# Filter spectra whose one differing row is stored from a tile of its own, and matrix casts queued behind the splits of the turned input

## The chip, the cores and the metric

The kernel runs on one core of one Trainium2 chip. The metric is device time in microseconds of one execution. Three runs of the kernel before gave 2880.81, 2882.52 and 2874.01 us. The profile is of a further execution that took 2877.9 us.

The engines are called as in the profile: PE is TensorE's matrix multiply and PEld its weight load, DVE is VectorE, ACT is ScalarE, POOL is GpSimd, SP is SyncE, which issues transfers and computes nothing. "SPq" is a DMA issued from SP.

## What is computed

Two layers of a diffusion backbone over 1024 latent tokens and 256 context tokens, 1024 channels. The change lies in the even layer's Hyena half: a short convolution, then two long convolutions with filters that a small network generates. Both become products of spectra:

```python
def long_conv(u, filt, skip):
    L = u.shape[1]
    uf = jnp.fft.rfft(u, n=2 * L, axis=1)
    ff = jnp.fft.rfft(filt, n=2 * L, axis=0)
    y = jnp.fft.irfft(uf * ff[None], n=2 * L, axis=1)[:, :L]
    return y + u * skip

def hyena_mix(p, conv_w, conv_b, w1, b1, freq, w2, b2, w3, skip):
    L = p.shape[1]
    z = short_conv(p, conv_w, conv_b).astype(jnp.float32)
    x1, x2, v = jnp.split(z, 3, axis=-1)
    filt = hyena_filters(L, w1, b1, freq, w2, b2, w3)
    skip = skip.astype(jnp.float32)
    v = x1 * long_conv(v, filt[:, 0], skip[0])
    v = x2 * long_conv(v, filt[:, 1], skip[1])
    return v.astype(p.dtype)
```

The other half of the channels goes through a two-dimensional Fourier transform; each layer ends with a SwiGLU feed-forward part, and the odd layer does neighbourhood attention.

## The kernel before, in words

All products run on PE as fp32 in two parts: `split` (L345 to L351) makes a rounded high part `hi` on ACT (L349) and the remainder `lo` on DVE (L351), and a product is three matrix multiplies, hi by hi, hi by lo and lo by hi. Nearly every matrix multiply goes through the helper `mm` (L345), every SP transfer through `ld` (L330), every POOL transfer through `ldr` (L336).

**Order.** The program is written with generators that hand out pieces of work between matrix multiplies, and is then ordered by a scheduler that simulates a timeline (`schedule_with_timeline_sim=True`). So a small edit can change the order of instructions far away. Each engine's instructions then run in that fixed order. `follow(ins)` adds an order, no wait: what is issued inside it comes later on its own engine than `ins`.

**Filter spectra**, up to about 445 us. For each of the two long convolutions (o = 0, 1) the filter is turned into a spectrum for the latent tokens (`spectrum_l`) and one for the context tokens (`spectrum_c`). This runs as filler beside the input projection, with `short_conv` (L1044 to L1048, on ACT and DVE) and the Fourier part of the context (L1504 to L1512) beside it. For each block of 128 rows by 512 channels ACT copies the sum from PSUM to a tile `t` (L1018 in `spectrum_l`, L911 in `spectrum_c`), and `ld(d[eo], t)` stores it to DRAM. One block of each spectrum is stored a second time, as `d[2]`, with its row 0 replaced by the row for the highest frequency, `fpi`. For that DVE overwrites row 0 of the same tile `t` (L1023, L914), and the whole tile is stored again. The overwrite has to wait until the first store of `t` has landed. This happens four times: in `spectrum_l` at 195 and 302 us, in `spectrum_c` at 364 and 444 us. `d[2]` is read much later, in the combination of the spectra (`fr2`).

**The turned input.** After the spectra, `turned()` transposes the short convolution's output on PE: eight groups of four transposes (L1261), each group followed by `split` (ACT L349, DVE L351). Then eight calls of `unit(0, ...)` multiply the turned input by Fourier matrices. Such a matrix lies in DRAM as fp16, is loaded by SP into a `cs` tile and cast to fp32 by ACT: `cmat2` casts two matrices (L411), `cmat` one (L397). The first unit uses the split pairs as soon as they are there. `gate_rows` (L1277) and `turn_x` (L1288, L1290) prepare the gate of the same convolution beside it.

**SP's queue.** SP's DMAs are issued in order, and a transfer waits on SP for its operands, and for the landing of the SP transfer eight places earlier, whose semaphore it takes over. POOL's and ACT's queues do the same for a few other transfers.

Of the kernel before, what the change touches and what calls it, by code (L numbers as in the profile page):

```python
# [230 lines left out]
class Act:  # L231
# [3 lines left out]
    def __init__(self):  # L235
        self.t = {}
# [22 lines left out]
class Builder:  # L259
    def __init__(self, ctx, tc, a, out, taps=None, stop=None):  # L260
        self.tc, self.nc, self.a, self.out = tc, tc.nc, a, out
        self.taps, self.stop = taps, stop
        ent = ctx.enter_context
        self.cp = ent(tc.tile_pool(name="cp", bufs=1))
        self.p4 = ent(tc.tile_pool(name="p4", bufs=21))
        self.p2 = ent(tc.tile_pool(name="p2", bufs=35))
        self.pg = ent(tc.tile_pool(name="pg", bufs=4))
        self.pt = ent(tc.tile_pool(name="pt", bufs=6))
        self.pko = ent(tc.tile_pool(name="pk", bufs=4))
        self.pw = ent(tc.tile_pool(name="pw", bufs=2))  # L270
        self.pp = ent(tc.tile_pool(name="pp", bufs=6, space=bass.MemoryType.PSUM))
        self.pq = ent(tc.tile_pool(name="pq", bufs=2, space=bass.MemoryType.PSUM))
        self.dr = ent(tc.tile_pool(name="dr", bufs=1, space=bass.MemoryType.DRAM))
        self.pad(self.cp, PAD_C)
        self.k = self.mk = self.pk = 0
        self.mj = self.p3 = 0
        self.held = False
        self.banks = 8
        self.sq = {}

# [102 lines left out]
    def cmat(self, w, src, view=None, small=False, shift=False):  # L383

        if small:
            st, m = self.S2(F16), self.S2(F32R, w)
            self.ld(view(st[:, :w]) if view else st[:, :w], src)
            self.nc.scalar.copy(m, st[:, :w])
            return m
        st = self.W("ws", "cs", F16, w)  # L390
        self.ld(view(st) if view else st, src)
        if shift:
            self.mk ^= 1
            m = self.shifted(("wh", "wl")[self.mk], "mat", w)
        else:
            m = self.mat(w)
        self.nc.scalar.copy(m, st)  # L397
        return m

    def cmat2(self, src, shift=False):  # L400

        st = self.W("ws", "cs", F16, 2048)
        self.ld(st, src)
        out = []
        for j in (0, 1):
            if shift:
                self.mk ^= 1
                m = self.shifted(("wh", "wl")[self.mk], "mat")
            else:
                m = self.mat(1024)  # L410
            self.nc.scalar.copy(m, st[:, j * 1024:j * 1024 + 1024])  # L411
            out.append(m)
        return out

# [392 lines left out]
    def filter_sum(self, sq, o, raw):  # L807
# [40 lines left out]
        if sq == "c":  # L848
            nc.vector.scalar_tensor_tensor(kap, nrm, 0.5, self.skip[:, o * 4:o * 4 + 4], op0=MUL, op1=MUL)

    def spectrum_c(self, o, raw):
        nc, a = self.nc, self.a
        fe, fo, re = raw[(0, 0, 0)], raw[(0, 0, 1)], raw[(0, 1, 0)]
        tot = self.filter_sum("c", o, raw)
        fh = (self.S2(F32R), self.S2(F32R))
        nc.scalar.copy(fh[0][0:1, :], re[0:1, :])
        nc.vector.tensor_tensor(fh[1][0:1, :], re[0:1, :], fh[0][0:1, :].bitcast(F32), SUB)
        m0, m1 = self.mask[:, 0:1], self.mask[:, 1:2]
        alt, one = self.alt[:, 2:4], self.alt[0:1, 0:2]

        def operands():
            for i in range(4):
                if i == 0:
                    f0 = self.T()
                    nc.vector.tensor_copy(f0, fe)
                    nc.vector.tensor_tensor(f0[0:1, :], fe[0:1, :], fo[0:1, :], ADD)
                    nc.vector.tensor_scalar(f0[0:1, :], f0[0:1, :], 0.5, None, op0=MUL)
                f, r = raw[(0, 0, i // 2)], raw[(0, 1, i // 2)]
                t = self.T()
                if i == 0:  # L870
                    nc.vector.scalar_tensor_tensor(t, r, m0, f0, op0=MUL, op1=ADD)
                elif i == 1:
                    nc.vector.scalar_tensor_tensor(t, r, m1, f0, op0=MUL, op1=ADD)
                elif i == 3:
                    nc.vector.scalar_tensor_tensor(t, f, m0, r, op0=MUL, op1=ADD)
                else:
                    nc.gpsimd.tensor_tensor(t, f, r, SUB)
                xh, xl = self.S2(F32R), self.S2(F32R)
                self.split(t, xh, xl)
                mt = self.TK(F32R, 2 * P)  # L880
                self.ldr(mt, a["ff_c"][i, 0])
                yield xh, xl, mt
            yield None

        ops = operands()
        nxt = next(ops)
        yield
        for i in range(4):
            cls, eo = i % 2, i // 2
            if i == 0:  # L890
                fpi = self.PS()
            acc = self.PS()
            xh, xl, mt = nxt
            if i == 0:
                for j, x in enumerate((xh, xl)):
                    self.mm(fpi[0:2, :], alt, x, j == 0, False)
            nxt = next(ops)
            if i % 2 == 0:
                next(tot, None)
            self.mm(acc, mt[:, :P], xh, True, False)  # L900
            self.mm(acc, mt[:, :P], xl, False, False)
            self.mm(acc, mt[:, P:], xh, False, i != 0)
            if i == 0:
                for j in (0, 1):
                    self.mm(fpi[0:2, :], one, fh[j][0:1, :], False, j == 1)
                    self.mm(acc, self.sgn[0:1, 256:384], fh[j][0:1, :], False, j == 1)
            if ("c", o, cls, 0) not in self.frg:
                self.frg[("c", o, cls, 0)] = self.DR([3 if cls == 0 else 2, P, HC])
            d = self.frg[("c", o, cls, 0)]
            t = self.S2()  # L910
            nc.scalar.copy(t, acc)  # L911
            self.ld(d[eo], t)
            if i == 0:
                nc.vector.tensor_copy(t[0:1, :], fpi[0:1, :])  # L914
                self.ld(d[2], t)
            yield
        for _ in tot:
            pass

    def spectrum_l(self, o, raw, tot):  # L920

        nc, a = self.nc, self.a
        V = nc.vector
# [61 lines left out]
        for i in classes:  # L985
            cls, eo = i % 2, i // 2
            kept = []
            for p in (0, 1):
                if i + p == 0:
                    fpi = self.PS()  # L990
# [20 lines left out]
                for f in (0, 1):  # L1011
                    fb = 2 * p + f
                    if eo:
                        self.frg[("l", o, cls, fb)] = self.DR([3 if cls + fb == 0 else 2, P, HC])
                    d = self.frg[("l", o, cls, fb)]
                    if cls == 0 or p == 0:
                        t = self.S2()
                        nc.scalar.copy(t, accs[f])  # L1018
                        kept.append(t)
                    if cls == 0:  # L1020
                        self.ld(d[eo], t)
                        if i + fb == 0:
                            V.tensor_copy(t[0:1, :], fpi[0:1, :])  # L1023
                            self.ld(d[2], t)
                    elif p:
                        x, t = self.S2(), kept[f]
                        V.tensor_tensor(x, accs[f], t, ADD)
                        self.ld(self.frg[("l", o, 1, f)][eo], x)
                        V.tensor_tensor(t, *((t, accs[f]) if i == 1 else (accs[f], t)), SUB)
                        self.ld(d[eo], t)  # L1030
# [223 lines left out]
    def turned(self):  # L1254

        nc = self.nc
        self.tr = []
        for j in range(8):
            ps = self.PS()
            for cb in range(4):  # L1260
                last = nc.tensor.transpose(ps[:, cb * P:(cb + 1) * P], self.ab["l"][cb][:, j * P:(j + 1) * P], self.ident)  # L1261
            self.after_turned = last.ins
            hi, lo = self.S2(F32R), self.S2(F32R)
            self.split(ps, hi, lo)
            self.tr.append((hi, lo))
            yield

    def gate_rows(self, pc):
# [1607 lines left out]
```

## Time and profile before

| | |
|---|---|
| median of three runs | 2880.81 us (2874.01 to 2882.52) |
| profiled execution | 2877.9 us |
| its span, first to last instruction | 2876.1 us |
| PE busy | 2773.0 us, 96% |
| PEld busy | 2332.6 us, 81% |
| DVE busy | 2087.4 us, 73% |
| ACT busy | 1318.2 us, 46% |
| POOL busy | 545.1 us, 19% |
| mean granted TensorE clock | 0.980 |

Between the span and the profiled execution's own time lie 1.8 us that no instruction shows. PE is the bound on average, so a change counts where it lengthens or shortens the time in which PE stands or runs at a lower clock. In the timeline view a row gives the start, the time to the end of the group, the engine, the line, the operation, the tiles without their numbers and how many instructions were put together; the bracket is the idle time of the engine ahead of the row and what ended it.

### The profile page before, as it was taken

How to read it: one execution, taken by the hardware profiler on the slowest of the kernel's cores; microseconds unless marked ns; L12 is line 12 of the kernel's file. 1: busy time of each engine (PE TensorE's matmuls, PEld its weight loads, DVE VectorE, ACT ScalarE, POOL GpSimd, SP SyncE). 2: the span in 40 equal slices, each digit the busy share in tenths (PEclk: the TensorE clock that was granted, in tenths of full speed). 3: DMA queues.
4: the chain of work that ended last, by engine and by line, in shares of the span. 5: the costliest groups of instructions: out<-in, count | busy, mean ns of one | idle time of the engine just before them, and what ended most of it. 6: DMA issues, size and time to landing. Idle time of an engine off the chain costs nothing. (4 is left out here: it accounts for less than half of the span.)

```text
span 2876.1 us, 43702 instructions
## 1 busy us (share of the span) xinstructions
PE 2773.0 (96%) x15542; PEld 2332.6 (81%) x15542; DVE 2087.4 (73%) x3652; ACT 1318.2 (46%) x2270; POOL 545.1 (19%) x880
## 2 busy tenths in 40 slices
PE   6999899999999999999999999999999999999998
PEld 4867677788899888888888888888887788888887
DVE  6668787758787888966777537777777877765556
ACT  4434335543554333333455326777764533333434
POOL 2210234341001212222010002232222022112000
PEclk9999898999999999999999999999999999999999
DMA  7354546746556555658884436777866276434663
GB/s 266 119 170 164 161 130 201 236 153 238 203 186 218 195 202 194 217 189 330 309 312 152 146 123 158 189 175 186 228 212 225 101 251 223 154 110 166 230 196 133
DMA packets 298600, 557.35 MB, mean 194 GB/s; under 512 B 82056, under 2 KB 128842, under 8 KB 298382
## 3 DMA queue, kind: packets, MB, share of 16 engines
q1 hardware_dynamic: 234030, 364.19, 40.2%
q0 software_dynamic: 61504, 185.65, 18.4%
q10 hardware_dynamic: 2848, 4.72, 0.4%
q8 instruction: 123, 2.02, 0.3%
q14 instruction: 95, 0.78, 0.1%
HBM read 407.10 MB, written 119.80 MB: 183 GB/s over the span
## 5 line engine op out<-in xcount | busy, mean ns | idle before, releaser
L1908 PE MATMUL ps<-s,s 128*128 128x512 f32 x1976 | 489.0, 390 | 0.4 <-ACT g L1913 0.3
L1908 PEld LDWEIGHTS ps<-s,s 128*128 128x128 f32 x1976 | 371.7, 188 | 78.8 <-ACT g L1913 1.3
L345 PE MATMUL ps<-s,wh 128*128 128x256 f32 (+1 forms) x1784 | 412.1, 333 | 3.5 <-ACT s L349 1.1
L345 PEld LDWEIGHTS ps<-s,wh 128*128 128x128 f32 x1784 | 301.1, 192 | 38.5 <-ACT wh L349 2.1
L345 PE MATMUL ps<-s,wl 128*128 128x256 f32 (+1 forms) x892 | 275.1, 332 | 1.1 <-DVE wl L351 1.1
L351 DVE TENSOR_TENSOR wl<-ws,wh 128x1024 fp32r<-128x1024 f32 (+1 forms) x141 | 168.6, 1198 | 131.7 <-ACT wh L349 127.4
L2085 PE MATMUL ps<-s,s 128*128 128x512 f32 (+1 forms) x1000 | 259.7, 383 | 3.1 <-DVE s L351 3.0
L349 ACT CAST s<-s 128x1024 fp32r<-128x1024 f32 (+2 forms) x192 | 172.5, 927 | 192.6 <-DMA s<-d 177.2
L345 PE MATMUL pq<-s,wh 128*128 128x512 f32 (+1 forms) x840 | 256.1, 385 | 0.4 <-DVE s L914 0.4
L345 PE MATMUL ps<-s,s 128*128 128x65 f16 (+4 forms) x2748 | 229.6, 235 | 18.1 <-DMA s<-tk 12.3
L349 ACT CAST wh<-ws 128x1024 fp32r<-128x1024 f32 (+1 forms) x141 | 144.6, 1027 | 192.1 <-PE ps L345 86.4
L349 ACT CAST s<-t 128x512 fp32r<-128x512 f32 (+2 forms) x238 | 133.8, 582 | 213.5 <-PE ps L1908 71.4
L351 DVE TENSOR_TENSOR s<-s,s 128x1024 fp32r<-128x1024 f32 (+2 forms) x170 | 190.7, 1154 | 48.8 <-ACT s L349 46.3
L2085 PEld LDWEIGHTS ps<-s,s 128*128 128x128 f32 x1000 | 184.4, 188 | 41.2 <-DVE s L351 4.9
L351 DVE TENSOR_TENSOR s<-t,s 128x512 fp32r<-128x512 f32 (+2 forms) x238 | 151.2, 651 | 74.7 <-ACT s L349 53.1
L1908 PE MATMUL ps<-s,wh 128*128 128x512 f32 x616 | 191.3, 390 | 0.0
L345 PEld LDWEIGHTS ps<-s,wl 128*128 128x128 f32 x892 | 168.7, 192 | 19.3 <-DVE wl L351 2.4
L336 POOL DMA_DIRECT2D d<-s x186 | 101.5, 547 | 369.1 <-DVE s L1715 90.0
L345 PEld LDWEIGHTS pq<-s,wh 128*128 128x128 f32 x840 | 150.0, 190 | 22.2 <-DVE s L914 0.8
L345 PE MATMUL pq<-s,wl 128*128 128x512 f32 (+1 forms) x420 | 159.3, 379 | 0.0
L2085 PE MATMUL ps<-s 128*128 128x512 f32 (+1 forms) x500 | 150.8, 385 | 0.0
L345 PEld LDWEIGHTS ps<-s,s 128*128 128x128 f32 (+1 forms) x828 | 130.3, 193 | 22.8 <-issue 2.8
(491 smaller groups left out, 5557.3 us busy)
## 6 DMA issues: line engine op xcount, KB each, us to landing
s<-d SPq DMA_DIRECT2D x283, 256.0 KB, 3.9
d<-s POOLq DMA_DIRECT2D x170, 256.0 KB, 4.0
s<-in_down SPq DMA_DIRECT2D x150, 256.0 KB, 4.2
s<-in_ada_w POOLq DMA_DIRECT2D x64, 512.0 KB, 5.0
ws<-in_up SPq DMA_DIRECT2D x44, 512.0 KB, 3.8
d<-g POOLq DMA_DIRECT2D x86, 256.0 KB, 2.9
ws<-in_gate SPq DMA_DIRECT2D x42, 512.0 KB, 3.8
d<-tk POOLq DMA_DIRECT2D x66, 256.0 KB, 4.3
```

Of the source, the lines that this page charges most:

```text
L336: self.last_ldr = self.nc.gpsimd.dma_start(out, in_).ins
L345: self.last_mm = self.nc.tensor.matmul(o, l, r, start=st, stop=sp).ins
L349: self.last_hi = nc.scalar.copy(hi, src).ins
L351: self.last_lo = eng.tensor_tensor(lo, src, hi.bitcast(F32), SUB).ins
L1908: nc.tensor.matmul(ps, x[:, sl], y, start=first and j == 0 and x is wh and y is xh, stop=j == 3 and x is wl, skip_group_check=True)
L2085: m = nc.tensor.matmul(acc[j][:, c0:c1], x[:, sl], y[:, xs], start=first and k == 0, stop=last and k == 2, skip_group_check=True)
```

## The change

Two edits.

First, `other_row` makes the second stored copy without touching `t`. A `g` tile takes the row `fpi` (DVE, L857 after the change), rows 1 to 127 of `t` are stored to `d[2, 1:]`, and the row of its own to `d[2, 0:1]`. So at each of the four places the overwrite of `t` is gone, and one store of 128 rows becomes a store of 127 rows and one of 1 row.

Second, `turned()` notes the last `hi` of its splits, and the casts of `cmat` and `cmat2` are placed behind it on ACT. Before `turned()` there is nothing to place them behind.

```diff
@@ -275,6 +275,7 @@
+        self.turned_hi = None
@@ -394,7 +395,8 @@ (cmat)
-        self.nc.scalar.copy(m, st)
+        with self.follow(self.turned_hi):
+            self.nc.scalar.copy(m, st)
         return m
@@ -408,7 +410,8 @@ (cmat2)
-            self.nc.scalar.copy(m, st[:, j * 1024:j * 1024 + 1024])
+            with self.follow(self.turned_hi):
+                self.nc.scalar.copy(m, st[:, j * 1024:j * 1024 + 1024])
             out.append(m)
@@ -848,6 +851,13 @@
+    def other_row(self, d, t, fpi):
+
+        row = self.G()
+        self.nc.vector.tensor_copy(row[0:1, :], fpi[0:1, :])
+        self.ld(d[2, 1:], t[1:, :])
+        self.ld(d[2, 0:1], row[0:1, :])
+
@@ -911,8 +921,7 @@ (spectrum_c)
             if i == 0:
-                nc.vector.tensor_copy(t[0:1, :], fpi[0:1, :])
-                self.ld(d[2], t)
+                self.other_row(d, t, fpi)
@@ -1020,8 +1029,7 @@ (spectrum_l)
                         if i + fb == 0:
-                            V.tensor_copy(t[0:1, :], fpi[0:1, :])
-                            self.ld(d[2], t)
+                            self.other_row(d, t, fpi)
@@ -1263,6 +1271,7 @@ (turned)
             self.split(ps, hi, lo)
             self.tr.append((hi, lo))
+            self.turned_hi = self.last_hi
             yield
```

With its four more transfers SP has 1243 instead of 1239. Since the scheduler starts anew, other instructions move too: on PE the order differs from about 180 to 700 us and again in the last feed-forward part, from about 2440 us; between them it is the same.

The first place is SP in `spectrum_l` for o = 0, near 195 us. `d_398` is the spectrum, `s2_488` the tile `t`, the loads from `in_w3` bring the next filter weights (the array is called `in_w` in the profile). Before:

```order
L330 DMA d_398_1453<-s2_488_1780 128x512
L330 DMA s2_490_1788<-in_w3 128x512
L330 DMA s2_491_1790<-in_w3 128x512
L330 DMA d_401_1457<-s2_489_1785 128x512
L330 DMA d_398_1453<-s2_488_1780 128x512
```

And after the change:

```order
L331 DMA d_398_1453<-g_489_1783 1x512
L331 DMA d_398_1453<-s2_488_1780 128x512
L331 DMA d_398_1453<-s2_488_1780 127x512
L331 DMA s2_491_1790<-in_w3 128x512
L331 DMA s2_492_1792<-in_w3 128x512
```

The second store of the tile stood behind the two loads; its 127 rows now stand ahead of them.

The second place is SP in `spectrum_c` for o = 0, near 360 us. `d_872` (after: `d_874`) is the spectrum, `s2_885` (after: `s2_888`) the tile from which the Fourier part of the context works (DVE L1504, POOL L1506). Before:

```order
L330 DMA ws_958_3595<-in_w_in 128x1024
L330 DMA d_872_3238<-s2_874_3239 128x512
L330 DMA s2_885_3300<-d_91_293 128x256
L330 DMA d_872_3238<-s2_874_3239 128x512
L330 DMA ws_978_3688<-in_ada_w 128x1024
```

And after the change:

```order
L331 DMA ws_961_3601<-in_w_in 128x1024
L331 DMA d_874_3242<-g_877_3246 1x512
L331 DMA d_874_3242<-s2_876_3243 128x512
L331 DMA d_874_3242<-s2_876_3243 127x512
L331 DMA s2_888_3306<-d_91_293 128x256
L331 DMA ws_981_3694<-in_ada_w 128x1024
```

Here too the store of 127 rows has moved ahead of a load that stood before it.

The third place is ACT around the turned input, near 450 us. `mat<-cs` are the matrix casts, `s2<-ps` the `hi` parts of the eight turned splits, `s2<-pq` and `s2_1087<-ps` (L911) the copies of the last two spectrum blocks. Before:

```order
L411 CAST mat_1174_4429<-cs_1173_4427 128x1024
L411 CAST mat_1175_4431<-cs_1173_4427 128x1024
L911 COPY s2_1085_4152<-pq_1073_4124 128x512
L911 COPY s2_1087_4159<-ps_1086_4155 128x512
L349 CAST s2_773_2863<-s2_937_3503 128x256 x2
L349 CAST s2_775_2865<-s2_1023_3894 128x256 x2
L349 CAST s2_1099_4201<-ps_1098_4196 128x512
L411 CAST mat_1197_4517<-cs_1196_4515 128x1024
L349 CAST s2_1102_4210<-ps_1101_4205 128x512
L349 CAST s2_1105_4219<-ps_1104_4214 128x512
```

And after the change, from the second of those two copies on:

```order
L921 COPY s2_1091_4167<-ps_1090_4163 128x512
L350 CAST s2_775_2867<-s2_940_3509 128x256 x2
L350 CAST s2_777_2869<-s2_1026_3900 128x256 x2
L350 CAST s2_1103_4209<-ps_1102_4204 128x512
L350 CAST s2_1106_4218<-ps_1105_4213 128x512
L350 CAST s2_1109_4227<-ps_1108_4222 128x512
L350 CAST s2_1112_4236<-ps_1111_4231 128x512
L350 CAST s2_1115_4245<-ps_1114_4240 128x512
L350 CAST s2_1118_4254<-ps_1117_4249 128x512
L350 CAST s2_1121_4263<-ps_1120_4258 128x512
L350 CAST s2_1124_4272<-ps_1123_4267 128x512
L414 CAST mat_1178_4437<-cs_1177_4435 128x1024
```

All casts of matrices have moved behind the eighth turned split. At this place SP's order has changed as well: the store of 127 rows of the last spectrum stands ahead of one of `gate_rows`' four loads and of the matrix loads.

## The prediction

> **What bounds the kernel now.** I read the page first, then the timeline at the four places where the row is overwritten and at the turned input, then the busy time and clock by stretches, and the DMA table last. The page says that PE is the bound, and its slices say where it is not at its full clock:
>
> ```profile
> span 2876.1 us, 43702 instructions
> PE 2773.0 (96%) x15542; PEld 2332.6 (81%) x15542; DVE 2087.4 (73%) x3652; ACT 1318.2 (46%) x2270; POOL 545.1 (19%) x880
> PEclk9999898999999999999999999999999999999999
> ```
>
> PE stands for 2876.1 - 2773.0 = 103 us in all. Both edits act before 500 us, the only part in which slices below 9 in the clock occur. So the change can only be worth some of those waits, and what the clock loses behind them. Which engine waits for the overwritten row is in the view of that source line and in the timeline. For `spectrum_c`:
>
> ```profile
> L914 DVE COPY s<-pq x1: 679/679/679, 363.7 to 363.7; 1x512 f32<-1x512 f32 x1
> L914 DVE COPY s<-ps x1: 678/678/678, 444.3 to 444.3; 1x512 f32<-1x512 f32 x1
>   DMA d<-s: 6.7, 2
>   PEld pq L345: 0.8, 1
>   PE pq L345: 0.4, 1
> ```
>
> DVE stands 6.7 us in two waits for the store's landing, and PE gets only 0.4 us of that directly. In `spectrum_l` the first of the two waits is as long:
>
> ```profile
> 193.30 0.87 SPq L330 DMA_DIRECT2D s<-in_w  x2
> 195.07 0.68 DVE L1023 COPY s<-ps 1x512 f32<-1x512 f32 x1 [6.52 <-DMA d<-s]
> 198.84 1.29 DVE L779 TENSOR_TENSOR t<-s,s 128x512 f32<-128x512 f32 x2 [1.40 <-DMA s<-in_w]
> 211.92 0.69 DVE L1027 TENSOR_TENSOR s<-ps,s 128x512 f32<-128x512 f32 x1 [6.92 <-PE ps L345]
> ```
>
> DVE waits 6.52 us for the landing, then 1.40 us for the loads from `in_w`, and stands again 6.92 us for PE before 211.92. The turned input is where PE stands:
>
> ```profile
> 450.16 2.00 ACT L411 CAST mat<-cs 128x1024 fp32r<-128x1024 f16 x2 [4.68 <-DMA cs<-in_vfo_l]
> 457.42 1.04 ACT L411 CAST mat<-cs 128x1024 fp32r<-128x1024 f16 x1 [2.33 <-DMA cs<-in_vfo_l]
> 458.98 4.28 DVE L351 TENSOR_TENSOR s<-ps,s 128x512 fp32r<-128x512 f32 x7 [3.17 <-ACT s L349]
> 459.73 1.12 PE L1261 MATMUL ps<-c,s 128*128 128x128 f32 x4 [3.21 <-DVE s L351]
> 462.20 4.86 PE L345 MATMUL ps<-s,mat 128*128 128x512 f32 x15
> 468.48 1.75 PE L345 MATMUL ps<-s,mat 128*128 128x512 f32 x7
> ```
>
> The third cast (457.42) waits 2.33 us for its matrix, with seven turned splits behind it on ACT. DVE's `lo` parts wait 3.17 us for those, the next transposes 3.21 us for DVE. The clock in these stretches:
>
> ```profile
> 355.00:364.00 9.00, 9.00 (x45) 6.73 (x44) 4.37 (x12) 1.87 (x3) 0.59 (x1) 1.00 0.41 117
> 364.00:380.00 16.00, 13.72 (x81) 11.63 (x81) 15.77 (x35) 4.75 (x13) 7.73 (x7) 0.98 0.24 74
> 443.00:462.20 19.20, 12.43 (x55) 9.97 (x55) 14.72 (x40) 12.03 (x24) 0.00 (x0) 0.62 0.75 221
> 462.20:480.00 17.80, 17.80 (x77) 14.69 (x76) 12.69 (x16) 6.29 (x10) 8.51 (x6) 0.93 0.66 212
> ```
>
> The columns are the stretch, its length, busy time of PE, PEld, DVE, ACT and POOL, the granted clock, the DMA share and GB/s. From 443 to 462.2 PE is busy for 12.43 of 19.20 us at a clock of 0.62. [...]
>
> **The new store, which decides the sum.** No store of 127 rows is in this trace. Its neighbours in the DMA table (KB each, median us to landing; then queue, packets, MB, share of 16 engines):
>
> ```profile
> d<-s SPq DMA_DIRECT2D x60, 256.0 KB, 3.0
> s<-in_zf SPq DMA_DIRECT2D x1, 165.0 KB
> s<-in_skiprow SPq DMA_DIRECT2D x2, 2.0 KB
> q1 hardware_dynamic: 234030, 364.19, 40.2%
> ```
>
> Lower bound: 127 rows are spread like 128, and land in 3.0 us. Upper bound: 127 has no divisor but itself, so if rows are dealt out in equal shares, one DMA engine takes them all. The 16 engines moved 364.19 MB of SP's queue in 40.2% of 16 x 2876.1 us, which is 19.7 KB a us for one; 127 x 2 KB are 260 kB, so 13 us. During that time other SP transfers that need this engine queue behind. For equal shares speaks that the table closes the 128-row transfers on which my sum rests, but gives no landing for `in_zf` (66 rows) or `in_skiprow` (1 row): there something other than 16 equal shares ended. That is weak evidence, but it is all there is; I take 13 us and keep 3.0 us as a rival.
>
> [...] No row of this trace shows how many engines a transfer took. [...]
>
> **Part by part, with 13 us.** Removed: four overwrites of 0.68 us on DVE and the wait ahead of them. Added: four copies of the same size, four 1-row stores, which I cost at nothing: SP issues them in about 0.4 us and none is read soon.
>
> *spectrum_l, 195 us: +4.* The 127-row store now stands ahead of the loads from `in_w`. Issued at about 193.3, it holds one engine until about 206.5, so the loads are late by 206.5 + 1 - 198.84 = 8.7 us, and DVE with them. DVE's later idle time covers 6.92 of that, so 1.8 us is left if PE never waits in between, 8.7 us if it waits at once. DVE's short convolution stands behind L779 and frees PSUM banks that PE wants; I take 4.
>
> *spectrum_l, 302 us: +1.5.* The second place has DVE idle nowhere near:
>
> ```profile
> 301.32 0.41 SPq L330 DMA_DIRECT2D ws<-in_w_in  x1
> 301.86 0.67 DVE L1023 COPY s<-ps 1x512 f32<-1x512 f32 x1
> 305.95 1.05 ACT L349 CAST wh<-ws 128x1024 fp32r<-128x1024 f32 x1
> 307.04 1.23 DVE L351 TENSOR_TENSOR wl<-ws,wh 128x1024 fp32r<-128x1024 f32 x1 [0.82 <-ACT wh L349]
> 313.44 1.43 DVE L1027 TENSOR_TENSOR s<-ps,s 128x512 f32<-128x512 f32 x2 [5.18 <-PE ps L345]
> ```
>
> Nothing is gained. The load of `ws` lands at about 300 + 13 = 313 instead of before 305.95; cast and remainder follow 7 us later, of which 5.18 was idle: 1.8 us late at the most, 0 if PE has other work. I take 1.5.
>
> *spectrum_c, 364 us: +5.* Here DVE is busy 15.77 of 16 us, and PE follows it:
>
> ```profile
> 359.81 0.37 SPq L330 DMA_DIRECT2D s<-d  x1
> 362.98 1.05 ACT L349 CAST wh<-ws 128x1024 fp32r<-128x1024 f32 x1 [4.78 <-DMA ws<-in_w_in]
> 363.67 0.68 DVE L914 COPY s<-pq 1x512 f32<-1x512 f32 x1 [4.59 <-DMA d<-s]
> 364.11 1.90 POOL L1506 TENSOR_TENSOR t<-s 128x127 f32<-128x127 f32 x1 [7.18 <-DMA s<-d]
> 364.40 0.73 PE L345 MATMUL pq<-s,wh 128*128 128x512 f32 x2 [0.35 <-DVE s L914]
> 365.41 0.27 DVE L1504 TENSOR_TENSOR t<-s 128x127 f32<-128x127 f32 x1
> 386.02 1.05 ACT L349 CAST wh<-ws 128x1024 fp32r<-128x1024 f32 x1 [1.90 <-DMA ws<-in_w_in]
> ```
>
> DVE's wait of 4.59 us goes, but its next work, the remainder of the weights, needs ACT's cast, which ends at 362.98 + 1.05 = 364.03. So what PE can gain is 0.35 us. The load that L1504 and L1506 need is issued at 359.81 and there at 364.11; behind a store of 13 us issued just ahead of it, it lands at about 373. DVE is 373 - 365.4 = 7.6 us late with the short convolution behind it. DVE's next slack is the wait for `wh` cast at 386.02, some 1.9 us. Between 1.9 (PE finds other work, much as from 355 to 364, where it was busy throughout) and 7.6; 7.6 - 1.9 - 0.35 = 5.35, I take 5.
>
> *The turned input, 444 to 465 us: -5.* The second `spectrum_c` overwrite goes with its wait (6.7 - 4.59 = 2.1 us on DVE), which kept splits behind it. All matrix casts now stand behind the eight splits: the 2.00 us of L411 no longer precede the L911 copies, and the wait of 2.33 us plus 1.04 us no longer precede splits two to eight. That removes PE's 3.21 us, and brings the transposes forward by up to 2.0 us: 5.2 us in all. What comes late instead is the cast itself: unit 0 can't start before its matrix. That matrix was cast by 452.2, and needs two casts of 1.04 us behind the last split. With its load issued about 445 it is ready about the time that the splits end, so I charge nothing; a load held by a 13 us store issued near 439.5 lands at about 453, still ahead of the splits. If the clock no longer falls ahead of unit 0, its first 15 multiplies gain too: 4.86 / 15 = 0.324 us each against 1.75 / 7 = 0.250 us of the later ones, 1.1 us in all. Between -1 (the load late) and -6.3; I take -5.
>
> Elsewhere the order moves where PE is nearly full:
>
> ```profile
> 480.00:700.00 220.00, 208.94 (x1141) 178.46 (x1141) 161.33 (x264) 100.42 (x146) 84.78 (x90) 0.98 0.63 214
> 2440.00:2870.00 430.00, 425.56 (x1924) 352.64 (x1922) 250.36 (x329) 166.33 (x231) 41.51 (x77) 1.00 0.48 164
> ```
>
> There are 11.1 and 4.4 us of idle PE to win or lose; I take 0, and 3 us either way.
>
> Sum: 4 + 1.5 + 5 - 5 = +5.5 us. Against the profiled execution's 2877.9 that is 2883.4, against the median, 2880.81, 2886.3. The profiled execution lies inside the three runs' spread, so I forecast between the two, 2885.
>
> **The rivals.** *The 127 rows spread over the engines like 128.* Then nothing is late at the first two places, the third gives -0.35, the turned input its full -6.3: about -6.6, and 2880.81 - 6.6 = 2874, up to 3 us less with luck in the reordered parts. For it: the nearest row by size is the 3.0 us of `d<-s`. Against it: the missing landings. Chance 0.27; a little over half of it counts as faster.
>
> *The one-engine store also drops the clock.* At 195 and 364 us PE then stands for a stretch of some 4 to 5 us, and the clock halves as it does around the turned input. The price is worked out from the 443 to 462.2 row: at 0.62, 38% of the pace is missing, 12.43 x 0.38 = 4.7 us for each such stretch. Two of them: +5.5 + 9.4 = +15, so 2896. [...] For it: PE is at a clock of 0.98 to 1.00 in the 355 and 364 stretches now, so all of it can be lost. Against it: the filler work that PE has there. Chance 0.28.
>
> *The casts do not hold the splits up.* If the 3.21 us were due to something else, the second edit would do nothing, and the turned input would give only the 2.1 us of the overwrite: 4 + 1.5 + 5 - 2.1 = +8.4, 2889. Chance 0.05.
>
> **How the numbers follow.** About 0.3%, 8.6 us, is what a measurement of this kernel can tell from no change: faster means below 2872.2, slower above 2889.4. The forecast case has 0.40, of which 0.35 within, 0.04 above, 0.01 below. The rivals: 0.15 below and 0.12 within for the spread store, 0.26 above and 0.02 within for the clock, 0.02 above and 0.03 within for the casts. That makes 0.16 faster, 0.52 same, 0.32 slower. The forecast's own range, with each term at its bounds, is 2876 to 2892. For 8 in 10 the range has to reach into both rivals, from 2868 (part of the spread store's luck left out) to 2898.
>
> **What would show it.** In the profile after, the row that matters is the landing of what stands behind a 127-row store: DVE L782 waiting near 207 for loads from `in_w`, and L1513 near 373 for `s<-d`, would show one engine; both on time, near 199 and 365, would show that I was wrong about the store. Fewer waits at the transposes (L1269) and a start of unit 0 about 5 us earlier, against the work ahead of it, would show the second edit right. If PE's clock in these stretches is below 0.8, the second rival holds. A change of more than 3 us behind 2440 us would break the zero that I took there.

## The result, and the profile after

| | before | after |
|---|---|---|
| median, 9 runs each | 2880.81 us (2871.05 to 2887.10) | 2895.43 us (2888.86 to 2907.26) |
| ratio, 95% interval | | 1.0062 [1.0041, 1.0084] |
| profiled execution | 2877.9 us | 2888.86 us |
| PE busy of its span | 2773.0 of 2876.1 us | 2770.5 of 2887.1 us |

The change makes the kernel slower by 0.6%, some 15 to 18 us. The time forecast was 2885 us, within the 0.3% that I called no change; the result lies inside the range (2868 to 2898), but on its slow side, where I had put 0.32.

PE does as much work as before and stands 117 us instead of 103. The page of the kernel after shows where, in the clock row, whose slices are 72 us long: the third, fifth and sixth (144 to 217 and 289 to 433 us) read 8, 7 and 8, where before they read 9, 8 and 9. The seventh, around the turned input, reads 9, where it read 8.

```profile
PEclk9989789999999999999999999999999999999999
```

The timeline of the kernel after, at the first place in `spectrum_l` (start, time to the end of the group, engine, what, and in brackets the wait ahead and what ended it):

```profile
189.63 0.66 SPq L331 DMA_DIRECT2D d<-s  x2
190.39 5.74 SPq L331 DMA_DIRECT2D s<-in_w  x2
207.69 1.29 DVE L782 TENSOR_TENSOR t<-s,s 128x512 f32<-128x512 f32 x2 [13.50 <-DMA s<-in_w]
211.13 2.93 PE L346 MATMUL ps<-s,tk 128*128 128x512 f32 x6 [7.89 <-DVE s L1054]
```

The second of the two stores in the first row has the 127 rows. Before the change DVE waited 1.40 us for these loads. Now DVE waits 13.50 us, and PE 7.89 us for the short convolution behind it. SP takes longer as well: 5.74 us to issue the two loads, where it took 0.87 us before. At the first place in `spectrum_c`:

```profile
370.12 0.67 SPq L331 DMA_DIRECT2D d<-s  x2
370.89 4.54 SPq L331 DMA_DIRECT2D s<-d  x1
384.31 0.29 DVE L1513 TENSOR_TENSOR t<-s 128x127 f32<-128x127 f32 x1 [9.02 <-DMA s<-d]
386.89 0.80 PE L346 MATMUL ps<-s,wh 128*128 128x256 f32 x2 [7.55 <-DVE s L352]
```

The load issued right behind the store is used 13.4 us later; before, 359.81 to 364.11, it took 4.3 us. Of the 13.4 us, 4.54 us are SP's issue, which took 0.37 us before; what holds the issue back no run took apart. Between the two lies the second `spectrum_l` place, where the weights and a load from POOL's queue (`in_ff_l`) are late:

```profile
311.92 2.90 PE L346 MATMUL ps<-s,tk 128*128 128x512 f32 x6 [3.03 <-DMA tk<-in_ff_l]
323.00 1.05 ACT L350 CAST wh<-ws 128x1024 fp32r<-128x1024 f32 x1 [13.49 <-DMA ws<-in_w_in]
```

Before the change ACT did not wait for these weights, and PE waited 0.33 us for `in_ff_l`.

At the turned input the change does what it says: of the 3.21 us that PE waited before the last transposes, 0.84 us is left.

```profile
472.75 1.25 PE L1269 MATMUL ps<-c,s 128*128 128x128 f32 x8 [0.84 <-DVE s L352]
```

The stretches of the two long waits, and the part of each wait in which PE, DVE, ACT and POOL all stand (length, busy time of PE, PEld, DVE, ACT, POOL, granted clock, DMA share, GB/s):

```profile
205.00:215.00 10.00, 3.87 (x9) 3.09 (x10) 6.16 (x12) 0.59 (x1) 0.00 (x0) 0.51 0.11 40
374.00:400.00 26.00, 18.45 (x84) 16.82 (x83) 16.70 (x40) 4.73 (x13) 6.26 (x7) 0.67 0.16 50
204.00:207.00 3.00, 0.00 (x0) 0.00 (x0) 0.00 (x0) 0.00 (x0) 0.00 (x0) 0.70 0.07 25
380.00:384.00 4.00, 0.00 (x0) 0.00 (x0) 0.00 (x0) 0.00 (x0) 0.00 (x0) 0.84 0.07 26
```

Over the two stretches the granted clock is 0.51 and 0.67. And the DMA engines are nearly idle there, at 0.11 and 0.16 of their time, and at 0.07 while everything stands: 1 of 16 is 0.06. So about one engine is at work while all wait, and it moves 25 to 26 kB a us. The loads do not wait because much else is moved: it is 40 and 50 GB/s over the two stretches, where the kernel before moved 181 from 205 to 215 us.

### The profile page after: what moved, and what is told of

It reads as the page before. It is cut to its first block, busy times and chain, and to the rows that moved or that the text cites. A ratio compares the mean times of both kernels' runs of the same rounds, so it can differ in the third digit from the quotient of the medians.

```text
span 2887.1 us, 43699 instructions
## 1 busy us (share of the span) xinstructions
PE 2770.5 (96%) x15542; PEld 2332.0 (81%) x15542; DVE 2086.2 (72%) x3652; ACT 1318.6 (46%) x2270; POOL 540.7 (19%) x880
## 5 line engine op out<-in xcount | busy, mean ns | idle before, releaser
L346 PE MATMUL ps<-s,s 128*128 128x65 f16 (+4 forms) x2748 | 229.6, 235 | 16.0 <-DMA s<-tk 10.5
L346 PEld LDWEIGHTS pq<-s,wh 128*128 128x128 f32 x840 | 149.6, 189 | 21.7 <-ACT wh L350 0.4
```

Source lines behind the costliest of these rows:

```text
L346: self.last_mm = self.nc.tensor.matmul(o, l, r, start=st, stop=sp).ins
```

## The experiments

**Theory:** a store of 127 rows from SP goes through one DMA engine, and what SP loads behind it is late. **Rivals:** the scheduler's new order makes the loss; the missing overwrite or the larger number of SP transfers does; the moved casts do. All ratios below are to the kernel before, run beside each experiment on the same chip.

**1. The same 127 rows from POOL's queue.** DVE and ACT keep the changed kernel's order, PE too but for two instructions.

```diff
-        self.ld(d[2, 1:], t[1:, :])
+        self.ldr(d[2, 1:], t[1:, :])
```

> The whole change, but the 127-row store goes from POOL's queue; DVE's and ACT's order stays that of the changed kernel, PE's nearly. Theory (a 127-row store issued from SP occupies one DMA engine for some 13 to 17 us and SP's loads queue behind it): if POOL's queue spreads the 127 rows, the loads from in_w are there by 196 to 199 us, PE's wait of 7.89 us at 211 us and the one of 7.55 us at 387 us are gone, and the time is 14 to 20 us below the changed kernel's 2895, so 2875 to 2881. If POOL's queue puts them on one engine too, its own transfers wait and the time stays at 2890 to 2900. Rival (the new order, or the missing overwrite, makes the loss): the waits and the 2895 stay.

Measured: 2862.91 us, ratio 0.9962 [0.9948, 0.9977], faster than both kernels, and below the 2875 to 2881 expected. The DMA table of this run (KB, median us to landing) and the first place:

```profile
d<-s POOLq DMA_DIRECT2D x4, 254.0 KB, 4.3
199.02 1.29 DVE L782 TENSOR_TENSOR t<-s,s 128x512 f32<-128x512 f32 x2 [1.42 <-DMA s<-in_w]
206.00:213.00 7.00, 7.00 (x35) 5.82 (x34) 0.66 (x2) 2.22 (x4) 1.78 (x4) 1.00 0.40 132
```

From POOL the same bytes land in 4.3 us, the loads are on time, and there PE is busy throughout at full clock. So the order and the missing overwrite do not make the loss.

**2. 126 rows and 1 row, from SP.**

```diff
-        self.ld(d[2, 1:], t[1:, :])
+        self.ld(d[2, 1:127], t[1:127, :])
+        self.ld(d[2, 127:], t[127:, :])
```

> The whole change, but the 127 rows are stored as 126 rows and 1 row, both from SP; 126 divides by 14. Theory (the count of rows sets the number of DMA engines): the 126-row store lands like a 128-row one in about 3 us, the waits of 7.89 and 7.55 us go, and the time is 2875 to 2882. Rival (a store that begins in row 1 is slow, or more transfers hold up SP's ring of eight): the loss stays, 2893 to 2900, one transfer more at each place. Rival (the order): it stays too.

Measured: 2872.92 us, 0.9996 [0.9982, 1.0010]. The loss is gone, with more SP transfers than in the changed kernel. But the order moved as well here, so the next pair is the clean test.

**3 and 4. The cut one row higher or lower.** The two kernels have the same order on PE, DVE, ACT and POOL as each other and as the changed kernel; they differ in whether 112 or 113 rows go in one store.

```diff
-        self.ld(d[2, 1:], t[1:, :])
+        self.ld(d[2, 16:], t[16:, :])
+        self.ld(d[2, 1:16], t[1:16, :])
```

> The whole change, with the 127 rows stored from SP as rows 16 to 127 (112 rows, divisible by 16) and rows 1 to 15 (15 rows). PE, ACT, DVE and POOL keep the changed kernel's order exactly. Theory (the number of engines comes from the divisors of the row count, and late loads are the loss): no wait of 7 us at 211 and 387 us, time near the store from POOL, 2860 to 2868. Rival (the gain of the store from POOL came from taking transfers off SP): 2872 or more, like the 126 rows.

```diff
-        self.ld(d[2, 1:], t[1:, :])
+        self.ld(d[2, 15:], t[15:, :])
+        self.ld(d[2, 1:15], t[1:15, :])
```

> As the kernel with 112 and 15 rows, and with the same order on every engine, but the cut lies one row lower: 113 rows (prime) and 14 rows. Theory: the 113 rows go to one DMA engine, 113/127 of the time of the 127-row store; the waits at 211 and 387 us come back as 6 to 7 us each and the time is 2885 to 2895. Rival (how many engines is not a matter of divisors: 113 rows spread like 112): the same time as 112 rows, 2860 to 2868.

Measured: 112 rows 2869.30 us, 0.9972 [0.9958, 0.9986]; 113 rows 2901.07 us, 1.0079 [1.0057, 1.0100]. One row more in the store costs 32 us. Both times lie a little above the ranges expected. The 113-row kernel has the long waits again, each about 1 us shorter than with 127 rows:

```profile
210.37 1.22 PE L346 MATMUL ps<-s,tk 128*128 128x512 f32 x2 [6.69 <-DVE s L1055]
389.67 0.58 PE L346 MATMUL ps<-s,wh 128*128 128x256 f32 x1 [6.76 <-DVE s L352]
```

So the theory of these expectations, that the divisors of the row count set the number of engines, fits the four counts that were stored from SP: 112 and 126 rows (0.9972 and 0.9996), which divide by 16 and 14, and 113 and 127 rows (1.0079 and 1.0062), which are prime. No other count was tried for the large store, apart from the 128 of the kernel before. How many engines work shows for 127 rows alone, in the DMA share of 0.07, about one of 16, while all stand (above). The four stores of 112 rows, 229 kB each, landed in 3.4 us in the median, 67 kB a us, so by an estimate from the 25 to 26 kB a us above they took more than one engine; with 113 rows DVE waits 12.29 us for the loads from `in_w`. Why 127 rows from POOL's queue land in 4.3 us (experiment 1) no run shows.

**5. Half the bytes.** The left 256 columns of the 127 rows from SP, the right 256 from POOL.

```diff
-        self.ld(d[2, 1:], t[1:, :])
+        self.ld(d[2, 1:, 0:256], t[1:, 0:256])
+        self.ldr(d[2, 1:, 256:], t[1:, 256:])
```

> The whole change, with the 127 rows cut along the channels: 127 x 256 from SP, 127 x 256 from POOL. Theory (one engine, its time in proportion to the bytes): the loads behind it are 6 to 8 us earlier than in the changed kernel, the wait at 211 us falls from 7.9 to 0 to 2 us, the one at 387 us from 7.6 to 0 to 3 us: 2866 to 2880. Rival (the time is per row, not per byte): waits as in the changed kernel, 2890 or more.

Measured: 2872.90 us, 0.9988 [0.9972, 1.0004].

```profile
209.81 0.50 PE L346 MATMUL ps<-s,tk 128*128 128x512 f32 x1 [3.35 <-DVE s L1055]
373.14 0.79 PE L346 MATMUL ps<-s,wh 128*128 128x256 f32 x2 [2.99 <-DVE s L352]
```

The waits fall by 7.89 - 3.35 = 4.5 and 7.55 - 2.99 = 4.6 us for 130 kB less. So the waits fall with the bytes, but what is left at the first place, 3.35 us, is more than I expected (0 to 2 us). By an estimate from this difference one engine does about 130 / 4.5 = 29 kB a us, and 25 to 26 by the rows above in which about one works. So by this estimate 260 kB take some 10 us, not the 13 of the prediction.

**6. The store from ACT's queue.** PE, DVE and POOL keep the changed kernel's order to the instruction; ACT's `dma_start` takes the place of SP's.

```diff
-        self.ld(d[2, 1:], t[1:, :])
+        self.lda(d[2, 1:], t[1:, :])
```

> The whole change, but the 127-row store goes from ACT's queue; PE, DVE and POOL keep the changed kernel's order to the instruction. Theory A (SP's loads wait because they stand behind the store in the same queue of that DMA engine): ACT has a queue of its own, so the loads share the engine with the store instead of standing behind it, the waits of 7.9 and 7.6 us shrink to 0 to 3 us, and the time is 2863 to 2875, near the store from POOL. Theory B (the one engine itself is the bottleneck, whatever the queue): the loads still end with the store, waits of 5 to 8 us, 2885 to 2896.

Measured: 2886.97 us, 1.0058 [1.0039, 1.0077], so the time is that of theory B; the waits tell more.

```profile
191.62 0.96 SPq L331 DMA_DIRECT2D s<-in_w  x2
201.28 1.29 DVE L782 TENSOR_TENSOR t<-s,s 128x512 f32<-128x512 f32 x2 [5.56 <-DMA s<-in_w]
204.75 0.47 PE L346 MATMUL pq<-s,tk 128*128 128x512 f32 x1 [0.96 <-DVE s L1054]
306.28 1.19 PE L346 MATMUL ps<-s,tk 128*128 128x512 f32 x2 [5.58 <-DMA tk<-in_ff_l]
381.59 0.58 PE L346 MATMUL ps<-c,t 128*128 128x1 f32 x2 [5.12 <-DVE s L352]
```

At the first place a queue of its own helps as expected: SP issues the two loads in 0.96 us instead of 5.74, DVE waits 5.56 instead of 13.50 us for SP's loads, and PE 0.96 instead of 7.89. At the others PE still waits 5.58 and 5.12 us, and the total is hardly better. So standing behind the store in one queue is part of the loss. `in_ff_l` comes from POOL's queue, so it does not stand behind a store from ACT's; that it waits for the store's engine, and that this is the other part, is my reading, and no row shows which engine a transfer took. How the parts divide at each place I did not settle.

**7. The store's shape alone.** The kernel before, with its overwrite and its wait, stores 127 rows and 1 row of the same tile.

```diff
-                self.ld(d[2], t)
+                self.ld(d[2, 1:], t[1:, :])
+                self.ld(d[2, 0:1], t[0:1, :])
```

> The kernel before with its overwrite and its wait kept, but the second copy stored as 127 rows and 1 row. Theory (the row count alone makes the loss): late loads and PE waits of 7 to 8 us near 211 and 387 us, time 2895 to 2915. Rival (only the missing overwrite and the new order do it): 2876 to 2881.

Measured: 2911.62 us, 1.0132 [1.0109, 1.0154].

```profile
211.64 1.29 DVE L779 TENSOR_TENSOR t<-s,s 128x512 f32<-128x512 f32 x2 [13.41 <-DMA s<-in_w]
215.09 1.22 PE L345 MATMUL ps<-s,tk 128*128 128x512 f32 x2 [7.70 <-DVE s L1048]
```

The same two waits, though the overwrite is still there and the casts have not moved. So neither the missing overwrite nor the moved casts are needed for the loss. The scheduler's order changed here too, so the clean test of the shape stays the pair of 112 and 113 rows.

**8 and 9. Each half of the change alone.** The casts only, with the 128-row store; and the rows only.

```diff
-                self.other_row(d, t, fpi)
+                nc.vector.tensor_copy(t[0:1, :], fpi[0:1, :])
+                self.ld(d[2], t)
```

(and the same in `spectrum_l`)

> Only the casts are placed behind the turned splits; the overwritten row and the 128-row store stay as before. Theory: no one-engine store, so nothing is late before 440 us; the turned input gains 3 to 5 us: 2875 to 2878. Rival (the order that the scheduler finds costs the time, whatever the store is): slower than before, 2885 or more.

```diff
-        with self.follow(self.turned_hi):
-            self.nc.scalar.copy(m, st)
+        self.nc.scalar.copy(m, st)
```

(and the same in `cmat2`)

> Only the row in its own tile with the 127-row store from SP; casts as before. Theory: the waits of about 8 us at 211 and 387 us are there as in the changed kernel, and the gain at the turned input is missing or smaller: 2895 to 2901. Rival (the casts' new place makes the loss): about 2881 or below.

Measured: casts only 2875.04 us, 0.9999 [0.9986, 1.0012]; rows only 2911.47 us, 1.0131 [1.0112, 1.0150], more than the 2895 to 2901 expected. The 127 rows cost 1.3% alone, and the casts win half of that back: with them 1.0062. The rows-only timeline shows how:

```profile
479.08 1.99 ACT L412 CAST mat<-cs 128x1024 fp32r<-128x1024 f16 x2 [11.35 <-DMA cs<-in_vfo_l]
480.98 0.58 ACT L919 COPY s<-ps 128x512 f32<-128x512 f32 x1
481.61 0.69 PE L1267 MATMUL ps<-c,s 128*128 128x128 f32 x2 [9.42 <-ACT s L919]
488.17 1.11 PE L1267 MATMUL ps<-c,s 128*128 128x128 f32 x4 [3.74 <-DVE s L352]
```

The matrix is late behind the fourth 127-row store, its cast waits 11.35 us on ACT, and the copy of the last spectrum block waits behind the cast; PE stands 9.42 and 3.74 us. In the changed kernel, with the casts behind the turned splits, nobody stands behind that load: the same two casts start at 478.38 us without a wait.

**10. The rows only, stored from POOL.** What the casts are worth when nothing is late.

```diff
-        self.ld(d[2, 1:], t[1:, :])
+        self.ldr(d[2, 1:], t[1:, :])
-        with self.follow(self.turned_hi):
-            self.nc.scalar.copy(m, st)
+        self.nc.scalar.copy(m, st)
```

> The row in its own tile with the 127-row store from POOL's queue, casts not moved. Asks what the casts' new place is worth when nothing is late. If it removes only the waits that late matrices cause (ACT standing with a cast ahead of other copies), then little is lost without it: 2863 to 2868. If it is worth the 16 us that lie between rows alone with the SP store (2911) and the whole change (2895): 2875 to 2880. My theory: in between, the turned input loses 3 to 5 us, so 2866 to 2870.

Measured: 2870.25 us, 0.9994 [0.9981, 1.0007]. So, with the row tile, the casts are worth 0.9994 - 0.9962 = 0.3%, some 9 us, and with both intervals 4 to 15 us. In the time of the whole kernel neither half alone shows a gain, and both together gain 0.4%. The profiles, one execution of each kernel, show the turned input alone. In each of them 261 multiplies lie between the same multiply near 400 us, the one with a wait of 1.9 us, and the first multiply of unit 0:

| kernel | from | to | us |
|---|---|---|---|
| before | 403.07 | 462.20 | 59.1 |
| casts only (experiment 8) | 405.35 | 461.25 | 55.9 |
| rows only, from POOL (this one) | 401.69 | 460.67 | 59.0 |
| both, from POOL (experiment 1) | 395.93 | 449.41 | 53.5 |
| the changed kernel | 421.68 | 475.78 | 54.1 |
| rows only, from SP (experiment 9) | 423.99 | 491.42 | 67.4 |

The casts alone gain 3.2 us there, too little to show in the time, the row alone next to nothing, both 5.7 us. The waits show why. Here, with the casts where they were:

```profile
455.29 1.04 ACT L412 CAST mat<-cs 128x1024 fp32r<-128x1024 f16 x1 [3.61 <-DMA cs<-in_vfo_l]
450.50 2.82 PE L1267 MATMUL ps<-c,s 128*128 128x128 f32 x12 [1.62 <-ACT s L919]
457.60 1.97 PE L1267 MATMUL ps<-c,s 128*128 128x128 f32 x8 [4.27 <-DVE s L352]
```

And with the casts moved but the overwrite kept (experiment 8):

```profile
447.77 0.68 DVE L924 COPY s<-ps 1x512 f32<-1x512 f32 x1 [2.38 <-DMA d<-s]
448.74 0.80 PE L346 MATMUL ps<-s,tk 128*128 128x512 f32 x1 [1.79 <-ACT s L350]
459.36 1.25 PE L1271 MATMUL ps<-c,s 128*128 128x128 f32 x8 [1.47 <-DVE s L352]
```

Without the overwrite's wait the casts hold PE up, 4.27 and 1.62 us; without the casts ahead, the overwrite's wait still does, 1.79 us, and 1.47 us are left at the transposes. In experiment 1 the longest wait at the transposes is 1.60 us.

**11. A whole second tile, 128 rows from SP.**

```diff
-        row = self.G()
-        self.nc.vector.tensor_copy(row[0:1, :], fpi[0:1, :])
-        self.ld(d[2, 1:], t[1:, :])
-        self.ld(d[2, 0:1], row[0:1, :])
+        t2 = self.S2()
+        self.nc.scalar.copy(t2, t)
+        self.nc.vector.tensor_copy(t2[0:1, :], fpi[0:1, :])
+        self.ld(d[2], t2)
```

> The whole change, but instead of a row tile ACT copies the whole block into a second tile (0.6 us of ACT at each place), DVE overwrites row 0 there, and SP stores 128 rows. Theory: the odd row count was the only fault, so this equals the store from POOL, 2863 to 2870. Rival (the gain of the store from POOL comes from taking 4 transfers off SP's queue): no gain, 2872 to 2878.

Measured: 2875.26 us, 1.0010 [0.9994, 1.0025]. The loss is gone, as the theory has it, but the gain that I expected did not come. The rival's reason can't be it, since the 112-row kernel issues more from SP than the changed one and gains. The order of the instructions is another, and ACT has four more copies; which of these takes the 0.4% stays open.

## Why the prediction was right or wrong

*One DMA engine for 127 rows:* right, by the DMA share of 0.07 while all stand, about one of 16. The `in_w` loads were forecast for DVE near 207 us, and came at 207.69. The choice between 3.0 and 13 us was the right one, but luck had a part in it. The sign it rests on, that a table row without a landing is not in 16 equal shares, does not hold up: in the changed kernel the 128-row loads from `in_w` have no landing either, and in the 112-row run the store of 15 rows has one, 4.9 us. The time fits by luck too. The store was issued at 190.0 us and not at 193.3, so the loads came 17.7 us behind it instead of the 14 forecast, though its own bytes, by the estimate in experiment 5, take some 10 us of one engine and not 13. SP's issue of the first load, 4.83 us, and what the engine carries of other transfers may make the difference; no run took it apart.

*The places:* right in kind, and all too small. This is the step that failed: I let DVE's idle time and filler work cover most of the delay. The same two multiplies, 881 apart in both kernels, bound the three places; before the change they are:

```profile
184.20 0.40 PE L345 MATMUL ps<-s,c 128*2 128x512 f32 x1 [3.79 <-ACT s L349]
403.07 0.82 PE L345 MATMUL ps<-s,s 128*128 128x256 f32 x3 [1.86 <-DVE s L1595]
```

That is 218.9 us. In the changed kernel, by the first and the last row below, it is 240.6. So the three places cost 21.7 us together, where I had 4 + 1.5 + 5 = 10.5. The same five PE instructions in the changed kernel and in the 112-row kernel, whose order is the same, measure it:

```profile
181.12 0.47 PE L346 MATMUL ps<-s,c 128*2 128x512 f32 x1 [3.80 <-ACT s L350]
225.87 0.50 PE L346 MATMUL pq<-s,s 128*128 128x512 f32 x1 [0.82 <-DVE s L806]
293.04 0.41 PE L346 MATMUL ps<-s,c 128*2 128x512 f32 x1 [2.16 <-ACT s L350]
345.81 0.80 PE L346 MATMUL pq<-g,s 128*128 128x512 f32 x1 [1.55 <-DVE g L352]
421.68 0.58 PE L346 MATMUL ps<-s,s 128*128 128x256 f32 x1 [1.88 <-DVE s L1604]
```

```profile
184.04 1.31 PE L346 MATMUL ps<-s,c 128*2 128x512 f32 x2 [3.79 <-ACT s L350]
217.97 0.73 PE L346 MATMUL pq<-s,s 128*128 128x512 f32 x2 [0.87 <-DVE s L806]
289.54 0.39 PE L346 MATMUL ps<-s,c 128*2 128x512 f32 x1 [2.16 <-ACT s L350]
335.14 0.50 PE L346 MATMUL pq<-g,s 128*128 128x512 f32 x1 [1.79 <-DVE g L352]
401.98 1.23 PE L346 MATMUL ps<-s,s 128*128 128x256 f32 x4 [1.86 <-DVE s L1605]
```

With the first row as zero, the changed kernel is 10.8 us behind at the second, 6.4 at the third, 13.6 at the fourth, 22.6 at the fifth, and 2887.1 - 2867.9 + 2.9 = 22.1 at the end of the span. So 195 us cost 10.8 instead of +4; 302 us 13.6 - 6.4 = 7.2 instead of +1.5; 364 us 9.0 instead of +5. The 4.4 us between the second and the third row are lost in the 112-row run, where no store stands; what it was is told at the end. PE's wait of 7.89 us at the first place is near the end of my bounds (1.8 to 8.7) that stood for "PE waits at once". At 302 us PE's wait for `in_ff_l` is 3.03 us; the rest of the 7.2 us I did not take apart.

*The clock:* I kept the clock out of the sum and gave it to a rival, at 2896. Its sign came, clocks of 0.51 and 0.67 in the stretches shown above, and its time is next to the 2895 measured. But its sum is not what happened, so the match is partly luck: it had the three places at 10.5 us and the clock at 9.4, 4.7 for each of two stretches, while at the first and the third place most of the loss is the waits themselves, 7.9 of 10.8 and 7.6 of 9.0 us. The 112-row kernel at the same work:

```profile
208.00:216.00 8.00, 8.00 (x39) 6.66 (x39) 4.35 (x7) 2.68 (x4) 2.12 (x4) 1.00 0.80 226
363.00:378.00 15.00, 12.43 (x75) 10.63 (x74) 14.29 (x30) 4.90 (x12) 6.32 (x7) 0.98 0.23 70
```

Of the 10.8 us at the first place the clock explains 3.87 x (1 - 0.51) = 1.9 us behind it, an estimate from the row 205 to 215, and with the wait's 7.9 us 1 us stays open. In the trace before, the clock was at 0.50 behind the 3.21 us at the turned input (459.7 to 462 us), so waits of 8 us should have counted with it; leaving it out of the likeliest case was the second, smaller fault.

*The turned input, -5:* right. By the table in experiment 10 the stretch to unit 0 takes 54.1 us instead of 59.1, so 5.0 less. Both edits are needed for it: the casts alone gain 3.2 us, the row alone next to nothing. In the changed kernel the casts were worth 0.7%, because they also take late matrices out of others' way: without them the same stretch takes 67.4 us. The prediction saw casts hold the splits up by 2.33 us, but did not price what a matrix late behind the new store would do there, 11.35 us in the rows-only run.

*Elsewhere, 0:* from the fifth row above to the end of the span the changed kernel takes 2887.1 - 421.7 = 2465.4 us, the 112-row kernel 2867.9 - 402.0 = 2465.9. So the store costs nothing there in the sum. From the first multiply of unit 0 to the end of the span the kernel before takes 2413.9 us and the changed one 2411.3, within the 3 us either way of the prediction.

*The spread store, 2874 (chance 0.27):* what a store that lands in time gives was measured in experiments 1 and 3, 0.9962 and 0.9972, 8 to 11 us faster; the -6.6 was near.

## What to carry to other kernels

Before a transfer is cut, measure the row counts that are left: from SP, pieces of 112 and 126 rows cost nothing here (0.9972 and 0.9996), pieces of 113 and 127 rows 0.8% and 0.6%. A store of 128 rows landed in 3.0 us in the median before the change; the one of 127 takes, by the estimate above, some 10 us of one engine, and the new order put it ahead of loads that the bound engine needed. When a delay of several microseconds is set against "idle time" and "filler", take the end of the bounds at which the bound engine waits at once, and add what its clock loses (0.51 in the stretch at the first place). Two waits can hold up the same work: then removing one shows little, and only the pair a gain.

## What I had not expected of the hardware

The clock does not fall with every wait. The same instruction, with nearly the same wait ahead of it, in the 112-row kernel and in the changed kernel, and the stretch behind it in each:

```profile
253.23 0.50 PE L346 MATMUL ps<-s,tk 128*128 128x512 f32 x1 [1.71 <-ACT s L350]
252.00:264.00 12.00, 10.77 (x31) 6.83 (x32) 9.11 (x18) 2.93 (x5) 0.53 (x1) 0.60 0.15 45
```

```profile
261.50 0.50 PE L346 MATMUL ps<-s,tk 128*128 128x512 f32 x1 [1.75 <-ACT s L350]
260.00:272.00 12.00, 10.50 (x49) 7.62 (x50) 10.96 (x25) 3.21 (x5) 0.53 (x1) 1.00 0.23 66
```

Around 1.71 us of idle time the clock was 0.60 on average, around 1.75 us it stayed at 1.00; in 12 us the one run did 31 multiplies, the other 49. This is the 4.4 us above. Runs of one kernel differ by 7 to 24 us here, and such stretches may be part of why; no run tested that.

Nor does the clock need the longest wait at the turned input, 3.21 us, to fall. In the kernel before it was at 0.50 already behind one of 1.79 us:

```profile
445.53 0.80 PE L345 MATMUL ps<-s,tk 128*128 128x512 f32 x1 [1.79 <-ACT s L349]
446.00:452.00 6.00, 5.27 (x18) 3.77 (x18) 6.00 (x17) 1.84 (x2) 0.00 (x0) 0.50 0.38 119
```

How long a wait has to be before the clock falls no row shows.
